# Expert weights of a mixture of experts fetched in rows of 8 KB instead of 2 KB

## The chip, the cores and the metric

The kernel runs on one core of one Trainium2 chip. The metric is the device time of one execution in microseconds, the median of several runs. The five engines are TensorE (PE; its weight loads are listed as PEld), VectorE (DVE), ScalarE (ACT), GpSimd (POOL) and SyncE (SP). SP issues nearly all transfers between the chip's memory and SBUF; they run on 16 DMA engines.

## What is computed

Two transformer blocks follow each other on 256 tokens of 1024 channels, in fp32. The first block ends in a mixture of 32 experts, two of them chosen for each token, and that is the part which matters here. Cut to it:

```python
h2 = modulate(rmsnorm(x, norm2_g), sh_m, sc_m)
# hier_moe: a group of 8 experts for each token, then the best 2 of its 8; gates of all others are 0
def body(acc, inp):
    wi, wo, ge = inp                       # (1024, 512), (256, 1024), (256,)
    a, u = jnp.split(t @ wi, 2, axis=-1)
    return acc + ((jax.nn.silu(a) * u) @ wo) * ge[:, None], None
y, _ = lax.scan(body, zeros, (w_expert_in, w_expert_out, gates))
x = x + gt_m * y
```

`w_expert_in` is (32, 1024, 512) and `w_expert_out` (32, 256, 1024) in fp32: 67 MB and 34 MB, all of which are read. Before this stands a token mixer (gated linear attention and pooling); behind it a second block with two FFNs, sparse attention, retention and a gate.

## The kernel before

**Stages.** The trace has them in this order: the modulation rows from `w_ada` and the projections of the first block (to about 140 us), its output projection `down(w_out)` and the routing (to about 197), the experts (to about 441), then the second block. In nearly all stages weights are read once, in tiles of 1 MB named `raw`, split into a rounded part `hi` (ACT, L197) and a rest `lo` (DVE, L198), and multiplied in two or three passes (L293 to L335).

**Memory.** SBUF is shared out by hand. `gp4` is a pool of eleven buffers of 4 KB a partition for temporaries (`t4`). Weight buffers lie in two regions, left and right, that `weight_pools` (L101) lays out anew between stages; a buffer of a new layout waits for the buffers of the old one on whose bytes it lies. `g4` in it are side buffers of the size of `gp4`'s, reached by `t4x`. `turn_of` takes the buffers of a kind in rotation.

**Experts.** Experts go in 11 units of three (the last has two). For each unit SP fetches twelve tiles `mw` of three experts by 128 rows by 512 columns, 6 KB a partition: eight tiles of `w_expert_in`, one for each block k of 128 channels, and four of `w_expert_out`, by column half n and block k (`unit_loads`, L704). Each row that is fetched is 2 KB. There are sixteen such buffers, 96 KB a partition. Five tiles of unit 0 are asked for early, from `ahead` (L775) in the middle of `down(w_out)`; the other eleven buffers lie over the left `raw`, `hi`, `lo` and `g4` of the stage before, `gta` in `g4` among them, which `x1_tile` reads. SP issues in order, so a load whose buffer isn't free holds all that stand behind it.

**Routing.** `x1_tile` and `logits` make the routing logits, DVE turns them into slots, and `gather_parts` (L825) writes the normed rows as a rounded part and a rest. Each expert takes up to 32 tokens. `gather` (L1027) multiplies the rows by a one-hot matrix `p4`, so that `xg` has the channels on partitions and the slots of a unit's four places side by side.

**One unit.** `in_proj` (L1065) multiplies, for each of eight k, four column groups of 32 (three experts and one place for an expert that overflows, chosen by a register). 32 of the trace's L1073 instructions are one half, kh. `act` is silu and product, `turn` transposes, `out_proj` (L1089) multiplies by the four `w_expert_out` tiles, `scatter` (L1098) spreads the result back over the tokens and adds it in PSUM. The gather of later units runs between. `scatter` of unit q stands behind `in_proj` of unit q+1. At q == 5 stands `beyond` (L973): a branch on whether an expert overflowed twice, passed by every engine.

**Behind the experts.** The left region gets `raw`, `hi`, `lo` and `g4` again, over the expert tiles' bytes, for the FFN (L1259), whose `hh` uses three side buffers.

Of the kernel before, what the change touches and what calls it, by code (L numbers as in the profile page):

```python
# [81 lines left out]
def body(ctx: ExitStack, tc: tile.TileContext, I, out, dbg=None):  # L82
# [6 lines left out]
    gp4 = ctx.enter_context(tc.tile_pool(name="gp4", bufs=11))  # L89
# [9 lines left out]
    SHAPES = {"g4": ([P, 1024], F32), "raw": ([P, 2048], F32), "hi": ([P, 1024], F32R), "lo": ([P, 1024], F32R), "mw": ([P, 3, 512], F32)}  # L99
# [24 lines left out]
    weight_pools("left", ("raw", 3), ("hi", 4), ("lo", 4), ("g4", 3))  # L124
# [127 lines left out]
    vrow = t1("vrow")[:44, :P]  # L252
# [6 lines left out]
    nc.scalar.dma_start(vrow[36:44, :], I["norm2_g"][0].rearrange("(k p) -> k p", p=P))  # L259
# [8 lines left out]
    vT = cp.tile([P, 44], F32, name="vT")  # L268
    sT = cp.tile([P, KD, 32], F32, name="sT")
    ps = bank()  # L270
    nc.tensor.transpose(ps[:, :44], vrow, ident[:44, :44])
    V.tensor_copy(vT, ps[:, :44])
# [7 lines left out]
    g2T = vT[:, 36:44]  # L280
# [418 lines left out]
    def unit_load(src, e):  # L699
        t = weight("mw")  # L700
        nc.sync.dma_start(t[:, :len(e)], src.rearrange("e p f -> p e f"))
        return t

    def unit_loads(u, some=12):  # L704
        e = experts[u]
        a, b = e[0], e[-1] + 1
        for k in range(KD):
            if k < some and (u, k) not in wi:
                wi[u, k] = unit_load(I["w_expert_in"][0, a:b, k * P:(k + 1) * P, :], e)
        for n in range(2):  # L710
            for k in range(2):
                if 8 + 2 * n + k < some and (u, k, n) not in wo:
                    wo[u, k, n] = unit_load(I["w_expert_out"][0, a:b, k * P:(k + 1) * P, n * 512:(n + 1) * 512], e)
# [3 lines left out]
    nc.sync.dma_start(wr[:, :, 0:4], I["w_router_group"][0].rearrange("(k p) f -> p k f", p=P))  # L717
    nc.sync.dma_start(wr[:, :, 8:40], I["w_router_expert"][0].rearrange("(k p) f -> p k f", p=P))
# [3 lines left out]
    def columns():  # L722
# [10 lines left out]
        for k in range(4):  # L733
            nc.tensor.transpose(pb[:, k * P:(k + 1) * P], row[:, k * P:(k + 1) * P], ident)
# [37 lines left out]
    weight_pools("right", ("mw", 5))  # L772
    pg = tok_panel((xL,), w_in, 1024, 512, (0, 0), ada_some)

    def ahead():  # L775
        columns()
        with after(asked):
            unit_loads(0, 5)
# [25 lines left out]
    def x1_tile(t):  # L804
# [3 lines left out]
        for n in range(2):  # L808
# [38 lines left out]
    weight_pools("left", ("mw", 4), ("mw", 5), ("mw", 2))  # L847
# [125 lines left out]
    def beyond():  # L973

        over = nc.values_load(mosti[0:1, 0:1], min_val=0, max_val=256)
        with tc.If(over > 0):  # L976
# [10 lines left out]
            with tc.For_i(0, NE, 1) as e:  # L987
                excess = nc.values_load(loads[0:1, bass.ds(e, 1)], min_val=0, max_val=256)
                with tc.If(excess > 0):
                    e_in, e_out = I["w_expert_in"][0, bass.ds(e, 1)][0], I["w_expert_out"][0, bass.ds(e, 1)][0]  # L990
                    pair_ = [bank(), bank()]
                    for c in range(2):
                        for m in range(2):
                            part = t4("part").rearrange("p (k f) -> p k f", k=KD)
                            c0 = 256 * c + P * m
                            nc.sync.dma_start(part, e_in[:, c0:c0 + P].rearrange("(k p) f -> p k f", p=P))
# [60 lines left out]
    def tiles_of(q, w):  # L1057

        if q == NU - 1:
# [5 lines left out]
    def in_proj(st_, q, kh):  # L1065
# [104 lines left out]
    weight_pools("left", ("raw", 5), ("hi", 6), ("lo", 6), ("g4", 3))  # L1170
# [88 lines left out]
    def ffn(norm, wg, wu, wdn):  # L1259

        hh, _ = blocks("hh", 22, F32R, 3)
# [196 lines left out]
    pT = [(t4x if i < 3 else t4)("pT").rearrange("p (h k q) -> p h k q", h=2, k=2) for i in range(4)]  # L1458
# [87 lines left out]
    yr = blocks2("yr", KD, 3)  # L1546
# [142 lines left out]
```

## Time and profile before

| | us |
|---|---|
| median of 3 runs (1098.5 to 1102.08) | 1098.74 |
| the profiled execution | 1098.91 |
| its span, first to last instruction | 1096.8 |

| engine | busy us | share |
|---|---|---|
| PE | 999.6 | 91% |
| PEld | 734.8 | 67% |
| DVE | 646.7 | 59% |
| ACT | 491.2 | 45% |

The profile page cuts the span into 40 slices of 27.4 us and gives for each the busy share of every engine, the clock that TensorE was granted, and what the DMA engines moved. A share for the whole span is an average over stages with different limits, so the stages have to be looked at one by one. Matmul instructions overlap in PE's pipeline; an instruction's duration is longer than the distance to the next one.

### The profile page before, as it was taken

The numbers are of one execution on the slowest core, as the hardware profiler recorded it, in microseconds if no ns is written. First come the engines' busy times: TensorE is split into PE (matmuls) and PEld (weight loads), VectorE is DVE, ScalarE is ACT, GpSimd is POOL, SyncE is SP. The second block draws the span as 40 slices with busy tenths as digits, with TensorE's granted clock in tenths as the row PEclk, the third lists the DMA queues.
The fourth block names the chain that finished last, engine by engine and source line by source line (L and its number), as shares of the span: only waits on it lengthen the run. The fifth ranks groups of instructions, "written<-read, shape, count | busy, mean of one in ns | idle before, by whom it ended". The sixth has DMA issues, their size and how long they took to land.

```text
span 1096.8 us, 15386 instructions
## 1 busy us (share of the span) xinstructions
PE 999.6 (91%) x5785; PEld 734.8 (67%) x5786; DVE 646.7 (59%) x1258; ACT 491.2 (45%) x873; POOL 5.7 (1%) x14
## 2 busy tenths in 40 slices
PE   4799997997778688799999999999999999999997
PEld 1586776442233132788888877787888788888886
DVE  3893865232112122976775499868659676775466
ACT  3544354321112011755554355675556455554353
POOL 1000000000000000000000000000000000000000
PEclk8899999999999989899999999999999999999999
DMA  9785886899999999776555633365367466565521
GB/s 374 270 298 182 304 289 220 307 385 386 387 383 386 386 387 381 239 238 193 184 219 192 192 117 114 118 209 167 102 206 253 128 196 223 159 222 197 190 81 39
DMA packets 152002, 260.60 MB, mean 238 GB/s; under 512 B 8444, under 2 KB 75240, under 8 KB 150648
## 3 DMA queue, kind: packets, MB, share of 16 engines
q1 hardware_dynamic: 151696, 259.32, 68.1%
q8 instruction: 48, 0.79, 0.3%
q10 hardware_dynamic: 232, 0.28, 0.1%
q14 instruction: 26, 0.21, 0.1%
HBM read 258.54 MB, written 1.05 MB: 237 GB/s over the span
## 4 chain that ended last, share of the span: by engine, by line
PE 59%; DMA 5%; DVE 4%; ACT 2%; issue 1%; DVEq 0%; ACTq 0%
PE mm L311 19%; PE mm L313 9%; PE acc L333 4%; PE acc L335 4%; PE acc L331 4%; DMA mw<-in_w_expert_in_dram 3%; PE acc L1237 2%; PE acc L1236 2%; PE acc L1244 2%; PE mm L1073 2%; PE mm L1095 2%; PE acc L294 1%; PE acc L295 1%; PE acc L293 1%; DMA mw<-in_w_expert_out_dram 1%; PE mm L1024 1%
## 5 line engine op out<-in xcount | busy, mean ns | idle before, releaser
L198 DVE TENSOR_TENSOR lo<-raw,hi 128x1024 fp32r<-128x1024 f32 (+1 forms) x240 | 287.2, 1204 | 159.6 <-ACT hi L197 157.0
L197 ACT CAST hi<-raw 128x1024 fp32r<-128x1024 f32 (+1 forms) x240 | 246.9, 1036 | 219.4 <-PE mm L311 93.6
L311 PE MATMUL mm<-xT,hi 128*128 128x512 f32 x832 | 211.9, 396 | 0.6 <-DVE rs L1516 0.6
L311 PEld LDWEIGHTS mm<-xT,hi 128*128 128x128 f32 x832 | 148.7, 188 | 28.5 <-DVE rs L1516 1.0
L313 PEld LDWEIGHTS mm<-xT,lo 128*128 128x128 f32 x832 | 110.6, 188 | 9.4
L313 PE MATMUL mm<-xT,lo 128*128 128x256 f32 x832 | 112.2, 277 | 0.0
L1073 PE MATMUL mm<-mw,xg 128*32 (+1 forms) x704 | 88.9, 600 | 21.6 <-DMA mw<-in_w_expert_in_dram 20.6
L1073 PEld LDWEIGHTS mm<-mw,xg 128*32 128x32 f32 x704 | 17.3, 109 | 71.9 <-DMA mw<-in_w_expert_in_dram 40.2
L295 PE MATMUL acc<-lo,xT 128*128 128x512 f32 x144 | 57.2, 402 | 1.9 <-DVE lo L198 1.9
L293 PE MATMUL acc<-hi,xT 128*128 128x512 f32 x144 | 58.3, 406 | 0.0
L294 PE MATMUL acc<-hi,xT 128*128 128x512 f32 x144 | 57.8, 401 | 0.0
L335 PE MATMUL acc<-lo,hh 128*128 128x512 f32 x176 | 56.3, 393 | 0.0
L333 PE MATMUL acc<-hi,hl 128*128 128x512 f32 x176 | 56.0, 392 | 0.0
L331 PE MATMUL acc<-hi,hh 128*128 128x512 f32 x176 | 55.9, 391 | 0.0
L1038 ACT ACTIVATE xg<-mm,shT,gmT 128x256 f32<-128x256 f32 (+1 forms) x48 | 23.4, 545 | 70.4 <-PE mm L1024 70.3
L1095 PE MATMUL mm<-mw,z 128*32 128x512 f32 (+1 forms) x352 | 46.5, 635 | 4.9 <-DMA mw<-in_w_expert_out_dram 4.4
L1103 DVE TENSOR_TENSOR og<-mm,gtm 128x512 f32<-128x512 f32 x22 | 15.2, 690 | 47.2 <-PE mm L1095 47.2
L1078 ACT ACTIVATE esg<-mm 128x256 f32<-128x256 f32 x11 | 4.2, 383 | 83.0 <-PE mm L1073 83.0
L1024 PE MATMUL mm<-p,xT 128*128 128x256 f32 (+1 forms) x192 | 34.7, 323 | 6.2 <-PEq L976 3.7
L1236 PE MATMUL acc<-hi,xT 128*128 128x256 f32 (+1 forms) x120 | 36.5, 330 | 2.3 <-ACT xT L197 2.3
L333 PEld LDWEIGHTS acc<-hi,hl 128*128 128x128 f32 x176 | 33.1, 188 | 7.3
L335 PEld LDWEIGHTS acc<-lo,hh 128*128 128x128 f32 x176 | 33.1, 188 | 7.2
(484 smaller groups left out, 1497.4 us busy)
## 6 DMA issues: line engine op xcount, KB each, us to landing
mw<-in_w_expert_in_dram SPq DMA_DIRECT2D x80, 768.0 KB, 13.0
raw<-in_w_in_dram SPq DMA_DIRECT2D x32, 1024.0 KB, 5.3
mw<-in_w_expert_out_dram SPq DMA_DIRECT2D x40, 768.0 KB, 13.1
raw<-in_w_ada_dram SPq DMA_DIRECT2D x24, 1024.0 KB, 8.4
raw<-in_ffn_w_gate_dram SPq DMA_DIRECT2D x22, 1024.0 KB, 5.5
raw<-in_ffn_w_up_dram SPq DMA_DIRECT2D x22, 1024.0 KB, 5.3
raw<-in_ffn_w_down_dram SPq DMA_DIRECT2D x22, 1024.0 KB, 4.9
raw<-in_w_out_dram SPq DMA_DIRECT2D x8, 1024.0 KB, 4.8
```

The source lines that it names most:

```text
L197: S.copy(hi, src)
L198: return V.tensor_tensor(lo, src, hi.bitcast(F32), op=ALU.subtract)
L293: mm(o, h_[k][:, c], hi[:, kk, z], start=k == starts, stop=False)
L294: mm(o, l_[k][:, c], hi[:, kk, z], start=False, stop=False)
L295: mm(o, h_[k][:, c], lo[:, kk, z], start=False, stop=k == stops)
L311: mm(pb, hi[:, k, :], x2[k], start=k == 0, stop=False, skip_group_check=True)
L313: mm(pb[:, 0:256], lo[:, k, :], x2[k][:, 0:256], start=False, stop=k == nk - 1, skip_group_check=True)
L331: mm(pa[t][n], hh[k][:, c], hi[:, 0, n * 512:(n + 1) * 512], start=k == seq[0], stop=False)
L333: mm(pa[t][n], hl[k][:, c], hi[:, 0, n * 512:(n + 1) * 512], start=False, stop=False)
L335: mm(pa[t][n], hh[k][:, c], lo[:, 0, n * 512:(n + 1) * 512], start=False, stop=k == seq[-1])
L1073: mm(st_["hp"][32 * i:32 * i + 32, :], xgs[q // 2][k // 4][:, k % 4, c:c + 32], w, start=k == 0, stop=k == KD - 1, skip_group_check=True)
L1095: mm(oo[n][r, :], st_["z"][:, k, r], w, start=k == 0, stop=k == 1, skip_group_check=True)
```

## The change

The tiles of expert weights become four times as large, 24 KB a partition, and there are four of them. Channels are renumbered inside each half of 512, so that partition p holds channels 4p to 4p+3: these are four neighbouring rows of `w_expert_in`, 8 KB in one piece. Inner units are renumbered alike, 2p and 2p+1, for `w_expert_out` (two rows of 4 KB in one piece). A unit has three tiles: two halves of `w_expert_in` and one of `w_expert_out`; only the second half of the last unit comes in four pieces of 512 columns. One tile instead of five small ones is asked for early.

All that meets the renumbered channels follows: the transposes of `xres` and of the modulation row take every fourth column, that of the hidden units every second, `gather_parts` writes its rows permuted in halves, the router weights come in two loads each, and `norm2_g` is fetched by its own transfer in place of eight rows of a transpose. `gp4` has one buffer less, the left region one side buffer more, and four lists of temporaries take one more tile from there.

```diff
-    gp4 = ctx.enter_context(tc.tile_pool(name="gp4", bufs=11))
+    gp4 = ctx.enter_context(tc.tile_pool(name="gp4", bufs=10))
...
-    SHAPES = {"g4": ([P, 1024], F32), "raw": ([P, 2048], F32), "hi": ([P, 1024], F32R), "lo": ([P, 1024], F32R), "mw": ([P, 3, 512], F32)}
+    SHAPES = {"g4": ([P, 1024], F32), "raw": ([P, 2048], F32), "hi": ([P, 1024], F32R), "lo": ([P, 1024], F32R), "mw": ([P, 3, 2 * D], F32)}
...
-    weight_pools("left", ("raw", 3), ("hi", 4), ("lo", 4), ("g4", 3))
+    weight_pools("left", ("raw", 3), ("hi", 4), ("lo", 4), ("g4", 4))
...
-    nc.scalar.dma_start(vrow[36:44, :], I["norm2_g"][0].rearrange("(k p) -> k p", p=P))
+    g2T = cp.tile([P, KD], F32, name="g2T")
+    nc.scalar.dma_start(g2T.rearrange("p (b k) -> p b k", k=4), I["norm2_g"][0].rearrange("(b p k) -> p b k", p=P, k=4))
...
-    def unit_load(src, e):
+    def unit_load(src, e, pieces=1):
         t = weight("mw")
-        nc.sync.dma_start(t[:, :len(e)], src.rearrange("e p f -> p e f"))
+        n = 2 * D // pieces
+        for c in range(0, 2 * D, n):
+            nc.sync.dma_start(t[:, :len(e), c:c + n], src[:, :, c:c + n])
         return t
...
-    def unit_loads(u, some=12):
+    def unit_loads(u, some=3):
+
         e = experts[u]
         a, b = e[0], e[-1] + 1
...
+        for h in range(2):
+            if h < some and (u, h) not in wi:
+                wi[u, h] = unit_load(I["w_expert_in"][0, a:b, 512 * h:512 * h + 512, :].rearrange(
+                    "e (p k) f -> p e (k f)", k=4), e, 4 if u == NU - 1 and h == 1 else 1)
+        if some > 2 and u not in wo:
+            wo[u] = unit_load(I["w_expert_out"][0, a:b].rearrange("e (p k) f -> p e (k f)", k=2), e)
+
+    def channels(k):
+
+        return slice(512 * (k // 4) + k % 4, 512 * (k // 4) + 512, 4)
...
+    for h in range(2):
+        for c, w in ((0, "w_router_group"), (8, "w_router_expert")):
+            n = I[w].shape[2]
+            nc.sync.dma_start(wr[:, 4 * h:4 * h + 4, c:c + n],
+                              I[w][0, 512 * h:512 * h + 512].rearrange("(p k) f -> p k f", k=4))
...
-    weight_pools("right", ("mw", 5))
+    weight_pools("right", ("mw", 1))
...
-            unit_loads(0, 5)
+            unit_loads(0, 1)
...
-                nc.tensor.transpose(pbs[n][:, kk * P:(kk + 1) * P], xres[:, t, k * P:(k + 1) * P], ident)
+                nc.tensor.transpose(pbs[n][:, kk * P:(kk + 1) * P], xres[:, t, channels(k)], ident)
...
-        S.activation(xrh[:, t, :], xres[:, t, :], AF.Copy, scale=rr[t])
-        V.scalar_tensor_tensor(xrl[:, t, :], xres[:, t, :], rr[t], xrh[:, t, :].bitcast(F32), op0=ALU.mult,
-                               op1=ALU.subtract)
+
+        for h in range(2):
+            c = slice(512 * h, 512 * h + 512)
+            src = xres[:, t, c].rearrange("p (c k) -> p k c", k=4)
+            S.activation(v4(xrh[:, t, c]), src, AF.Copy, scale=rr[t])
+            V.scalar_tensor_tensor(v4(xrl[:, t, c]), src, rr[t], v4(xrh[:, t, c]).bitcast(F32), op0=ALU.mult,
+                                   op1=ALU.subtract)
...
-    weight_pools("left", ("mw", 4), ("mw", 5), ("mw", 2))
+    weight_pools("left", ("mw", 1), ("mw", 2))
...
-            for i, w in enumerate(tiles_of(q, wi[q, k])):
+            for i, w in enumerate(tiles_of(q, wi[q, k // 4], (k % 4) * 512)):
...
-            nc.tensor.transpose(tp[:, k * P:(k + 1) * P], st_["sg"][:, k * P:(k + 1) * P], ident)
+            nc.tensor.transpose(tp[:, k * P:(k + 1) * P], st_["sg"][:, k:256:2], ident)
...
-                for i, w in enumerate(tiles_of(q, wo[q, k, n])):
+                for i, w in enumerate(tiles_of(q, wo[q], k * D + n * 512)):
...
-    weight_pools("left", ("raw", 5), ("hi", 6), ("lo", 6), ("g4", 3))
+    weight_pools("left", ("raw", 5), ("hi", 6), ("lo", 6), ("g4", 4))
...
-        hh, _ = blocks("hh", 22, F32R, 3)
+        hh, _ = blocks("hh", 22, F32R, 4)
```

## Rows read from the trace of the kernel before

**Rows 1.** The page's 40 slices of the span: PE busy tenths, DMA, GB/s.

```profile
PE   4799997997778688799999999999999999999997
...
DMA  9785886899999999776555633365367466565521
GB/s 374 270 298 182 304 289 220 307 385 386 387 383 386 386 387 381 239 238 193 184 219 192 192 117 114 118 209 167 102 206 253 128 196 223 159 222 197 190 81 39
```

**Rows 2.** Waits in 215:440: who waited for whom, us in total, times, longest.

```profile
PE mm L1073 <- DMA mw<-in_w_expert_in_dram: 20.6, 27, 1.2
```

**Rows 3.** Stretches: length, busy us (x instructions) by engine, PEclk, DMA share, GB/s.

```profile
16.00:24.00 8.00, 4.67 (x14) 2.54 (x15) 4.42 (x23) 6.90 (x15) 2.59 (x4) 0.62 1.02 430
16.00:28.00 12.00, 8.30 (x36) 4.04 (x36) 7.13 (x30) 8.05 (x16) 2.83 (x4) 0.72 1.02 427
114.00:120.00 6.00, 5.36 (x35) 4.03 (x34) 5.45 (x10) 2.00 (x2) 0.00 (x0) 1.00 1.03 412
230.00:300.00 70.00, 55.65 (x382) 20.96 (x378) 13.86 (x28) 10.97 (x21) 0.00 (x0) 0.98 1.05 387
320.00:420.00 100.00, 79.39 (x542) 28.80 (x538) 21.78 (x42) 15.96 (x31) 0.00 (x0) 0.97 1.05 387
440.00:446.00 6.00, 1.46 (x6) 0.88 (x6) 5.21 (x16) 5.19 (x17) 0.00 (x0) 0.89 1.10 348
...
380.00:400.00 20.00, 15.74 (x79) 5.70 (x80) 4.55 (x8) 4.16 (x9) 0.00 (x0) 0.83 1.05 388
```

**Rows 4.** Transfers: packets by size; an issue's start and us; KB and us to landing.

```profile
DMA packets 152002, 260.60 MB, mean 238 GB/s; under 512 B 8444, under 2 KB 75240, under 8 KB 150648
...
10.80 5.53 SPq L169 DMA_DIRECT2D raw<-in_w_ada_dram  x5
...
raw<-in_retmat_dram SPq DMA_DIRECT2D x1, 1024.0 KB, 4.8
...
DMA to landing us min/median/max: 5.4/12.9/14.7
```

**Rows 5.** PE in order of time, units 0 to 3: start us, us, instructions, count.

```profile
197.54 7.07 PE L1073 MATMUL mm<-mw,xg 128*32 x64
...
215.98 3.64 PE L1095 MATMUL mm<-mw,z 128*32 x32
...
227.38 2.76 PE L1073 MATMUL mm<-mw,xg 128*32 x24
...
247.30 1.07 PE L1073 MATMUL mm<-mw,xg 128*32 x8 [0.62 <-DMA mw<-in_w_expert_in_dram]
```

**Rows 6.** SP's queue in order of time, before and in the first units.

```profile
166.88 0.90 SPq L701 DMA_DIRECT2D mw<-in_w_expert_in_dram  x2
...
181.58 0.49 SPq L701 DMA_DIRECT2D mw<-in_w_expert_out_dram  x1
...
217.10 8.34 SPq L701 DMA_DIRECT2D mw<-in_w_expert_in_dram  x8
```

**Rows 7.** PE and SP around the branch at L976, in order of time.

```profile
310.32 1.06 PE L1073 MATMUL mm<-mw,xg 128*32 x8 [0.98 <-SPq L976]
...
314.83 8.88 SPq L701 DMA_DIRECT2D mw<-in_w_expert_in_dram  x8
...
315.06 2.05 PE L1024 MATMUL mm<-p,xT 128*128 128x256 f32 x8 [3.68 <-PEq L976]
```

**Rows 8.** PE in order of time: unit 8, then the last unit's end.

```profile
388.89 5.02 PE L1095 MATMUL mm<-mw,z 128*32 x24
...
433.10 2.78 PE L1095 MATMUL mm<-mw,z 128*32 128x512 f32 x24 [0.52 <-DVE z L1087]
...
440.17 0.73 PE L1110 MATMUL acc<-ol,back 128*128 128x512 f32 x2
```

**Rows 9.** DVE in order of time at the routing, token tile 0, then 1.

```profile
179.58 1.28 DVE L827 SCALAR_TENSOR_TENSOR xT<-xres,rmsz,xT 128x1024 fp32r<-128x1024 f32 x1 [0.69 <-ACT xT L826]
180.88 0.69 DVE L810 TENSOR_TENSOR om<-acc,ada 128x512 f32<-128x512 f32 x1
```

More of the change, by code (lines that the diff above doesn't have):

```diff
@@ L251, in body @@
     LF, LB, SF, SB, AFW = (tri[:, i * P:(i + 1) * P] for i in range(5))
-    vrow = t1("vrow")[:44, :P]
+    vrow = t1("vrow")[:36, :P]
     nc.scalar.dma_start(vrow[0:8, :], I["c"][0].rearrange("(k p) -> k p", p=P))
@@ L267, in body @@
     CI = cp.tile([P, 2, 32], F32R, name="CI")
-    vT = cp.tile([P, 44], F32, name="vT")
+    vT = cp.tile([P, 36], F32, name="vT")
     sT = cp.tile([P, KD, 32], F32, name="sT")
     ps = bank()
-    nc.tensor.transpose(ps[:, :44], vrow, ident[:44, :44])
-    V.tensor_copy(vT, ps[:, :44])
+    nc.tensor.transpose(ps[:, :36], vrow, ident[:36, :36])
+    V.tensor_copy(vT, ps[:, :36])
     V.tensor_copy(cstr, cst[:, 0:3, :])
@@ L279, in body @@
     rgnT = vT[:, 28:36]
-    g2T = vT[:, 36:44]
     def tok_mm(pa, lhs, w, c0, n, starts, stops, kh, skip=(0, 0)):
@@ L697, in body @@
     wi, wo = {}, {}
-    def unit_load(src, e):
+    def unit_load(src, e, pieces=1):
         t = weight("mw")
-        nc.sync.dma_start(t[:, :len(e)], src.rearrange("e p f -> p e f"))
+        n = 2 * D // pieces
+        for c in range(0, 2 * D, n):
+            nc.sync.dma_start(t[:, :len(e), c:c + n], src[:, :, c:c + n])
         return t
-    def unit_loads(u, some=12):
+    def unit_loads(u, some=3):
         e = experts[u]
         a, b = e[0], e[-1] + 1
[L707 to L713, printed above, removed]
+        for h in range(2):
[6 more added lines that the diff above has]
+        return slice(512 * (k // 4) + k % 4, 512 * (k // 4) + 512, 4)
     wr = t2("wr")[:, :KD * 40].rearrange("p (k f) -> p k f", k=KD)
     G.memset(wr, 0.0)
-    nc.sync.dma_start(wr[:, :, 0:4], I["w_router_group"][0].rearrange("(k p) f -> p k f", p=P))
-    nc.sync.dma_start(wr[:, :, 8:40], I["w_router_expert"][0].rearrange("(k p) f -> p k f", p=P))
+    for h in range(2):
[3 more added lines that the diff above has]
+                              I[w][0, 512 * h:512 * h + 512].rearrange("(p k) f -> p k f", k=4))
     shT, gmT, base = small(8, "shT", 1), small(8, "gmT", 1), small(40, "base", 1)
@@ L733, in columns @@
         for k in range(4):
-            nc.tensor.transpose(pb[:, k * P:(k + 1) * P], row[:, k * P:(k + 1) * P], ident)
+            nc.tensor.transpose(pb[:, k * P:(k + 1) * P], row[:, channels(k)], ident)
         cols = pb.rearrange("p (k j c) -> p c j k", j=4, c=32)
@@ L994, in beyond @@
                             part = t4("part").rearrange("p (k f) -> p k f", k=KD)
-                            c0 = 256 * c + P * m
-                            nc.sync.dma_start(part, e_in[:, c0:c0 + P].rearrange("(k p) f -> p k f", p=P))
+                            c0 = slice(256 * c + P * m, 256 * c + P * m + P)
+                            for h in range(2):
+                                nc.sync.dma_start(part[:, 4 * h:4 * h + 4, :], e_in[512 * h:512 * h + 512, c0]
+                                                  .rearrange("(p k) f -> p k f", k=4))
                             for k in range(KD):
@@ L1055, in way_back, with tiles_of @@
         return gs, back
-    def tiles_of(q, w):
+    def tiles_of(q, w, c0):
+        w = w[:, :, c0:c0 + 512]
         if q == NU - 1:
@@ L1455, in body @@
     rope_T(aqT, tok_panel((xL,), w2i, 0, 512)[0], 8, 32)
-    pT = [(t4x if i < 3 else t4)("pT").rearrange("p (h k q) -> p h k q", h=2, k=2) for i in range(4)]
+    pT = [(t4x if i < 4 else t4)("pT").rearrange("p (h k q) -> p h k q", h=2, k=2) for i in range(4)]
     for t in range(2):
@@ L1544, in pair @@
         return tiles[k2 // 2][:, 2 * (k2 % 2):2 * (k2 % 2) + 2, :]
-    yr = blocks2("yr", KD, 3)
+    yr = blocks2("yr", KD, 4)
     yr_ = [x.rearrange("p i c -> p (i c)") for x in yr]
@@ L1613, in body @@
     fg = row_bcast(t4x("fg"), I["final_norm_2"], D)
-    gt = [t4("gt"), t4("gt")]
+    gt = [t4x("gt"), t4("gt")]
     fss = small(6, "fss", 1).rearrange("p (t n) -> p t n", t=2)
```

## The prediction

> **What bounds the kernel now.** I read the 40 slices of the span first [rows 1]: two limits take turns. Through most of the span PE is at 9 tenths, but from about 220 to 440 us, the expert stage, the DMA line stands at 9 and 381 to 387 GB/s while PE falls to 6 to 8. So this stage, and this one alone, goes at the pace of the weight transfers. The table of waits says the same from PE's side: in 215:440 the expert matmuls of L1073 waited 27 times for `mw<-in_w_expert_in`, 20.6 us in all and none longer than 1.2 [rows 2]: each k tile comes just too late. Two long stretches show 387 GB/s at a DMA share of 1.05, PE busy 0.8 of the time [rows 3]. A change is worth something here if it moves the bytes faster or if it opens or closes gaps in that stream.
>
> **The rate by row length.** Other saturated stretches of this trace have other row lengths [rows 3]: 440:446, FFN panels of 256 columns (1 KB rows), 348 GB/s; 114:120, mostly 4 KB rows, 412; 16:28, 427. The last one is the five 1 MB loads of `w_ada` issued from 10.80 us on [rows 4], 2048 columns to a row, so 8 KB. The page counts 152002 packets, 150648 of them under 8 KB [rows 4], so 1354 of 8 KB or more: the eight `w_ada` loads alone have 1024 such rows, so a row of 8 KB does travel as one packet. In one order, 348, 387, 412, 427: longer rows are faster although all four stretches have the engines busy throughout.
>
> [...]
>
> **Removed and added: the stream.** A full tile becomes 3 x 128 rows x 8 KB = 3.146 MB, a unit three tiles, 9.437 MB as before. At 387 GB/s a tile takes 8.13 us and a unit 24.4; at 427, 7.37 and 22.1. I take 427, since it is measured on rows of the very length; the bounds are 387 (no gain) and 430, the first 8 us of the same loads (16:24) [rows 3].
>
> **Where the stream starts.** The same 96 KB of buffers hold four tiles instead of sixteen, and each is free only when its last reader is done. The early part, step by step: the first tile is asked for beside `w_out`, as five small ones are now. The second needs all three left `raw` buffers, free by about 168 us as now (SP issued small tiles there at 166.88) [rows 6]. The third and fourth lie over `hi`, `lo` and `gta`, which the last matmuls of L335 and x1_tile(1) hold: now SP gets through at 181.58 [rows 6], then too. They land before 198.5, and the fifth, h1 of unit 1, waits for the first half of in_proj(0): from 197.54 half of 7.07 us [rows 5], 201.1; with 2.3 us of latency (the 1 MB `retmat` load, 8 KB rows, landed in 4.8 us [rows 4]; 1.049 MB at 427 is 2.46) and 7.4 of transfer it lands at 210.8. in_proj(1) wants it near 209.8: 1 us of PE lost, out_proj(0) from 216.0 to 217 and its end from 219.6 to 220.4 [rows 5]. There the seventh tile (h0 of unit 2) is let in, behind which SP holds the rest; now SP goes on at 217.10 [rows 6]. So the gapless stream begins at 220.4 + 2.3 = 222.7, some 3 us later than now (217.10 + 2.3), with about as many bytes already in (six tiles, 18.9 MB). h0 of unit 2 lands at 230.1, where in_proj(2) now starts at 227.38 [rows 5]: PE idles there.
>
> **Where the stream ends.** From 222.7 on: 24 full tiles, 24 x 7.37 = 176.9; `fng`, 0.52 MB, 1.2; unit 10, two experts, two tiles of 2.10 MB at 4.91 and the four pieces of h1 that keep 2 KB rows, 5.42, together 15.2. That is 193.3 us, 416.0. One gap is added: at q == 5 every engine passes the branch of L976. Now PE ends in_proj(5) at 311.38 and goes on at 315.06, SP at 314.83, 3.45 us after PE's end [rows 7], and some 13 us of transfers asked for before (the median from issue to landing [rows 4]) cover it. After, only wo of unit 5 is asked for while SP stands there: h1 lands, PE needs 3.6 for its half, 3.45 for the branch, 2.3 until new bytes flow, 9.4 against the 7.4 of wo: 2.0 lost. So wo of unit 10 is in at 418.0.
>
> **The end of the stage.** Now out_proj(10) starts at 433.10 and the last scatter ends at 440.90: 7.8 us [rows 8], paced by PE with nothing waiting for weights. After, wo comes as one tile, so all of out_proj stands behind it, and PE may be 0.9 late from out_proj(9), scatter(9) and both halves of in_proj(10), which follow within 15 us: 418.0 + 0.9 + 7.8 = 426.7. The FFN panels follow the last weights in the queue as now and are wanted only after the norm behind the scatter, so their cover moves along. Gain: 440.9 - 426.7 = 14.2 us.
>
> **Can PE keep up?** From in_proj(2) to in_proj(3) is 227.38 to 247.30, 19.9 us [rows 5], with 2.3 us of idling in it: 17.6 us of work, 18.6 with the wait for esg that stays. That is under 22.1 and 16% spare. A tile let go late does not stop the stream soon: h0 is wanted again only 22 us after it landed, and PE needs 4 to 6. What is queued behind a late tile is all of SP; who waits is PE a unit later.
>
> **The small parts.** gather_parts becomes two DVE steps of 512 for one of 1024, 2 x 0.69 for 1.28 [rows 9], reading with a stride of 16 B; for token tile 0 L810 of x1_tile(1) is right behind it, so 0.1 us if the stride is free, 1.4 if it halves the rate; I take 0.2, since 512 and 1024 elements stand at 0.69 and 1.28 us, a time that goes by the elements. The strided transposes (two a unit, sixteen before the stage) change no count; zero to 0.5, in a stage with 3.5 us spare per unit. `g2T` adds 256 packets of 16 B to a start that is DMA bound: 0.2. The two more `wr` loads go out in the fourth slice, 82 to 110 us, at 182 GB/s with PE at 9 [rows 1], long before they are read: nothing. gp4 has one buffer less, and the tiles that are moved to the side pool (hh, pT, yr, gt) make up for it in the later stages; before 190 us and in the expert stage it is one less outright: 0 to 3, 0.5 taken, as I see no step there that needs the eleventh for long. Together 0.9.
>
> **Sum.** 14.2 - 0.9 = 13.3. The profiled execution took 1098.91 (span 1096.8 and 2.1 around it), 0.17 above the median of 1098.74, so nothing to correct: 1085.6.
>
> **Rivals.** 1. **The stream stays at 387 GB/s**, because memory or the cores' ports and not the packets set it; the coarse tiles then only cost. 82.3 MB at 387 is 212.7 us, from 222.7 to 435.4, with a smaller gap at the branch (1.3), 8.7 of tail and the small parts: 446.3, 5.4 late, 1104.3. It decides below 398 GB/s, where 82.3 MB fill just the time there is (440.9 less 222.7, 8.7, 2.0 and 0.9). Against it: 412 and 427 on the same engines; for it: all those stretches are short, and none reads three experts in turn. 0.10. 2. **PE becomes the bound**: waiting for whole tiles lets its clock fall. The granted clock was 0.83 in 380:400 [rows 3], after idling between tiles, and there 24 matmuls of L1095 took 5.02 us from 388.89 against 2.78 from 433.10 [rows 8]. One such group of 32 a unit adds 3.0 us, 21.6, still under 22.1; at two groups the unit is about 24.4 and the gain is gone. Halfway, 23.5 for eight units, costs 11: 1096. 0.10. 3. **Part of the rate only**, rows cut to 4 KB or the mix giving 412: 82.3 MB in 199.8 instead of 192.7, 1092.7; or the small parts at their upper bounds (4 more), 1090. 0.13. 4. Better: 430 GB/s (1.3 us), no gap at the branch (2.0), PE not late at the end (0.9), the small parts at nothing (0.9): 1080.5. 0.05.
>
> **How the numbers follow.** My forecast, 1082 to 1089, has 0.62. A measurement of this kernel tells 0.3%, 3.3 us, from no change. Faster: 0.62 + 0.13 + 0.05 and half of rival 2, 0.85. Slower: most of rival 1 and a little of 2, 0.09; the rest, 0.06, is the same. For 8 in 10 the range reaches from rival 4 to rival 2, 1080 to 1097, and leaves out rival 1.
>
> **What would show it.** DMA at 420 to 430 GB/s in the saturated stretch, packets of 8 KB or more up from 1354 by some 12000 (unit 10's pieces aside), units about 22 us apart at in_proj's starts, the last scatter near 427. A gap of 2 us in the DMA line behind L976, a PE wait before in_proj(2) of 2 to 3 us. Wrong would be: 387 GB/s with long packets (rival 1), DMA gaps in every unit with SP waiting for L1073 or L1095 (buffers too coarse), or PE without idling and a granted clock well under 0.9 there (rival 2).

## The result, and the profile after

| us | before | after |
|---|---|---|
| median of 9 runs each, taken together | 1099.3 (1096.54 to 1102.08) | 1091.38 (1089.36 to 1093.82) |
| profiled execution | 1098.91 | 1089.5 |
| its span | 1096.8 | 1087.2 |

The ratio is 0.993, 95% interval 0.9919 to 0.9941: 7.9 us faster. The forecast was 1085.6, with a range of 1080 to 1097; the time lies in it, but 2.4 us above the narrower 1082 to 1089. The direction and the main mechanism (longer rows, a faster stream) hold, and some 40% of the expected gain of 13.3 us is missing. The two profiled executions are 9.4 us apart; what follows is read from them.

The page's slices and packets of after:

```profile
PE   4799999898878787999999999999999999999996
...
DMA  9786866799989999665555542354367366555511
GB/s 377 275 293 190 305 235 251 293 422 419 422 361 420 422 420 370 211 207 183 205 213 192 157 165 97 130 189 155 117 205 260 120 213 200 173 215 210 187 68 39
DMA packets 114658, 260.59 MB, mean 240 GB/s; under 512 B 7205, under 2 KB 73993, under 8 KB 101273
```

Beside [rows 1] the expert stage is now at 419 to 422 GB/s where it stood at 381 to 387, but one slice of the stream stands out: 361 in the twelfth (299 to 326), where before had 383. The eighth (190 to 217), where the stream begins, has 293 for 307. Packets of 8 KB or more are 114658 - 101273 = 13385, against 1354 [rows 4], 12031 more, as forecast.

Stretches of after: length, busy us (x instructions) of PE, PEld, DVE, ACT and POOL, granted clock, DMA share, GB/s. Then who waited for weights in 215:435 (total us, times, longest).

```profile
184.00:192.00 8.00, 6.63 (x18) 3.94 (x17) 3.31 (x23) 4.64 (x5) 0.00 (x0) 0.50 1.01 428
196.00:204.00 8.00, 8.00 (x70) 4.85 (x72) 3.89 (x20) 5.20 (x10) 0.00 (x0) 0.93 0.07 26
206.00:210.00 4.00, 3.74 (x36) 1.31 (x32) 1.14 (x4) 0.38 (x1) 0.00 (x0) 1.00 0.99 420
240.00:300.00 60.00, 49.41 (x350) 19.93 (x346) 12.85 (x25) 10.74 (x21) 0.00 (x0) 0.94 1.01 420
306.00:314.00 8.00, 4.21 (x28) 2.79 (x21) 1.17 (x2) 0.80 (x2) 0.00 (x0) 0.74 0.60 219
308.00:310.00 2.00, 0.00 (x0) 0.00 (x0) 1.17 (x2) 0.16 (x1) 0.00 (x0) 0.95 0.75 299
310.00:312.00 2.00, 0.50 (x2) 0.53 (x3) 0.00 (x0) 0.00 (x0) 0.00 (x0) 0.50 0.17 66
340.00:380.00 40.00, 30.65 (x234) 11.61 (x226) 7.21 (x16) 5.39 (x12) 0.00 (x0) 0.96 1.01 421
...
PE mm L1089 <- DMA mw<-in_w_expert_in_dram: 9.0, 6, 3.8
PE mm L1111 <- DMA mw<-in_w_expert_out_dram: 4.9, 4, 1.5
```

The stream stands still until 204, runs at 420 from 206 on, loses 8 x (1 - 219/421) = 3.8 us in 306:314 and then runs at 421 again. PE waits for `w_expert_in` six times and 9.0 us instead of 27 times and 20.6 [rows 2], so less often but longer each time.

PE in order of time (start, us, instructions), L1089 being in_proj and L1111 out_proj; the last row is the end of the last scatter. Behind it, the first matmuls of the FFN, of after and then of before.

```profile
199.53 4.93 PE L1089 MATMUL mm<-mw,xg 128*32 x44
...
406.69 3.64 PE L1111 MATMUL mm<-mw,z 128*32 x32 [1.54 <-DMA mw<-in_w_expert_out_dram]
...
423.85 3.64 PE L1111 MATMUL mm<-mw,z 128*32 128x512 f32 x32 [0.52 <-DVE z L1103]
...
430.00 0.73 PE L1126 MATMUL acc<-ol,back 128*128 128x512 f32 x2
...
452.70 2.12 PE L311 MATMUL mm<-xT,hi 128*128 128x512 f32 x8
```

```profile
462.13 2.12 PE L311 MATMUL mm<-xT,hi 128*128 128x512 f32 x8
```

in_proj(0) starts at 199.53 against 197.54 [rows 5]. The last scatter ends at 430.73 against 440.90 [rows 8], 10.2 us earlier. The first L311 matmul of the FFN stands at 452.70 instead of 462.13, 9.4 earlier, and from it to the end of the span the kernels take 634.5 and 634.7 us. So the whole gain is made before 431, and 0.7 of it is lost between the last scatter and the FFN; why is open.

### The profile page after: what moved, and what is told of

Read it like the earlier page. It is cut to its first block, busy times and chain, and to the rows that moved or that the text cites. A ratio compares the mean times of both kernels' runs of the same rounds, so it can differ in the third digit from the quotient of the medians.

```text
span 1087.2 us, 15196 instructions
## 1 busy us (share of the span) xinstructions
PE 997.5 (92%) x5785; PEld 741.5 (68%) x5786; DVE 648.6 (60%) x1260; ACT 493.5 (45%) x875; POOL 5.7 (1%) x14
## 2 busy tenths in 40 slices
DMA packets 114658, 260.59 MB, mean 240 GB/s; under 512 B 7205, under 2 KB 73993, under 8 KB 101273
## 3 DMA queue, kind: packets, MB, share of 16 engines
HBM read 258.54 MB, written 1.05 MB: 239 GB/s over the span
## 4 chain that ended last, share of the span: by engine, by line
PE 58%; DMA 6%; DVE 4%; ACT 2%; issue 1%; SPq 0%; DVEq 0%; ACTq 0%
PE mm L311 20%; PE mm L313 9%; PE acc L333 4%; PE acc L335 4%; PE acc L331 4%; DMA mw<-in_w_expert_out_dram 3%; DMA mw<-in_w_expert_in_dram 2%; PE mm L1089 2%; PE acc L1253 2%; PE acc L1252 2%; PE acc L1260 2%; PE acc L294 1%; PE acc L295 1%; PE acc L293 1%; DMA raw<-in_ffn_w_up_dram 1%
## 5 line engine op out<-in xcount | busy, mean ns | idle before, releaser
L311 PE MATMUL mm<-xT,hi 128*128 128x512 f32 x832 | 211.8, 396 | 0.6 <-DVE rs L1532 0.6
L311 PEld LDWEIGHTS mm<-xT,hi 128*128 128x128 f32 x832 | 148.5, 188 | 28.6 <-DVE rs L1532 1.0
L1089 PE MATMUL mm<-mw,xg 128*32 (+1 forms) x704 | 85.8, 632 | 11.9 <-DMA mw<-in_w_expert_in_dram 10.9
L1089 PEld LDWEIGHTS mm<-mw,xg 128*32 128x32 f32 x704 | 22.2, 115 | 63.7 <-issue 52.4
L1111 PE MATMUL mm<-mw,z 128*32 128x512 f32 (+1 forms) x352 | 41.5, 601 | 5.5 <-DMA mw<-in_w_expert_out_dram 4.9
L331 PEld LDWEIGHTS acc<-hi,hh 128*128 128x128 f32 x176 | 32.9, 188 | 7.5
```

The costliest lines, as they stand in the source:

```text
L311: mm(pb, hi[:, k, :], x2[k], start=k == 0, stop=False, skip_group_check=True)
L331: mm(pa[t][n], hh[k][:, c], hi[:, 0, n * 512:(n + 1) * 512], start=k == seq[0], stop=False)
L1089: mm(st_["hp"][32 * i:32 * i + 32, :], xgs[q // 2][k // 4][:, k % 4, c:c + 32], w, start=k == 0, stop=k == KD - 1, skip_group_check=True)
```

## The experiments

My theory was the prediction's, with what the trace of after had added: rows of 8 KB make the rate, the branch makes the hole, the strided steps make in_proj(0) late. The rivals: the gain comes from larger tiles and not from longer rows; the hole is PE's standstill and costs nothing; PE sets the pace, so that nothing done to the stream shows. A difference under about 2 us between kernels of this list isn't told apart by their times alone.

**The changed kernel again**, on the chip of rows_2kb, two_tiles_ahead and plain_gather, which were run beside it.

> The changed kernel as it is, beside which the next three are read on the same chip. 0.993 of the kernel before, as measured; last scatter near 431 us, 420 GB/s in the expert stage, a hole of some 5 us in the transfers behind the branch at q == 5, in_proj(0) near 199.5 us.

1090.3 us, ratio 0.9906 (0.9891 to 0.9921). Its profile repeats that of after: 421 GB/s in 240:300, 336 in 300:320, in_proj(0) at 200.11, the last scatter's end at 431.36.

**Rows of 2 KB in the same tiles.** Only the cut of each load changes.

```diff
-                    "e (p k) f -> p e (k f)", k=4), e, 4 if u == NU - 1 and h == 1 else 1)
+                    "e (p k) f -> p e (k f)", k=4), e, 4)
...
-            wo[u] = unit_load(I["w_expert_out"][0, a:b].rearrange("e (p k) f -> p e (k f)", k=2), e)
+            wo[u] = unit_load(I["w_expert_out"][0, a:b].rearrange("e (p k) f -> p e (k f)", k=2), e, 4)
```

> The changed kernel with every expert tile fetched in four pieces of 512 columns: rows of 2 KB again, everything else (four large tiles, permuted channels, pools) as changed. Theory 1, the row length sets the rate and the rate the stage: 387 GB/s, 8.13 us a tile for 7.48; 26 tiles from 205 us on make 17 us more, last scatter near 447, time near 1108, slower than the kernel before. Rival, the gain is from fewer and larger tiles and fewer waits: 420 GB/s in the four-piece form too or no loss from 387, time near 1091.

1113.17 us, ratio 1.0112 (1.0093 to 1.0131). **Rows of 4 KB**, the same with 2 in place of the 4 and the last unit's second half left in four pieces:

> The changed kernel with every full tile asked for in two pieces of 1024 columns, rows of 4 KB; tiles, buffers and waits as in the changed kernel. By the rows of 114:120 (412 GB/s, mostly 4 KB rows) between the 386 of 2 KB and the 420 of 8 KB: 405 to 412 in 240:300, 7.7 us a tile, 24 tiles 4 to 6 us more, the last scatter near 436 and 1095 to 1096. If the rate has its step between 2 and 4 KB and not more beyond: 419 or more and within 1.5 us of the changed kernel.

1097.87 us, ratio 0.9982 (0.9967 to 0.9996). The stretch 240:300 of the two, 2 KB first (columns as above):

```profile
240.00:300.00 60.00, 46.38 (x316) 20.60 (x318) 10.53 (x22) 9.59 (x19) 0.00 (x0) 0.91 1.05 386
```

```profile
240.00:300.00 60.00, 45.83 (x333) 19.14 (x332) 12.86 (x25) 10.98 (x21) 0.00 (x0) 0.97 1.03 409
```

With one tile, one buffer and one matmul order for all three, the rate goes 386, 409, 420 with the length of the row: the first rival falls. It also shows what the coarse tiles cost by themselves: with 2 KB rows the kernel is 12.5 us slower than the one before on that chip (1100.68), at the same 386 to 387 GB/s. Longer rows give 22.9 back (1113.2 to 1090.3), and the change's gain is the difference.

**One load for each expert.** Each tile is asked for by three loads of 1.05 MB.

```diff
-            nc.sync.dma_start(t[:, :len(e), c:c + n], src[:, :, c:c + n])
+            for i in range(len(e)):
+                nc.sync.dma_start(t[:, i, c:c + n], src[:, i, c:c + n])
```

> The changed kernel, with each tile asked for by three loads of 1.05 MB (one expert each, 128 rows of 8 KB) instead of one of 3.15 MB; rows and bytes are the same. If the 420 to 421 GB/s against the 427 of the w_ada loads come from the three experts in one load (three rows a partition in turn): 427 in 240:300 and 340:360, 7.37 us a tile, 26 tiles 2.9 us less, the last scatter near 428.5 and 1088. If it is the state of the chip in this stage (PE, DVE and ACT at work beside it): 420 again, within 1 us of the changed kernel, 1090 to 1091.

1090.17 us, ratio 0.9903 (0.9886 to 0.9919), 420 GB/s in 240:300. Three experts in one load are not why 427 wasn't reached. That the work of the other engines beside the stream is, as the expectation's second case has it, isn't shown by this.

**Without the branch.** The two lines `if q == 5: beyond()` are left out, of the changed kernel and of the one before.

> The changed kernel with the call of beyond() left out: the overflow path (L986 to L1029) and the branch ahead of it are not there, which for this data leaves out no work that is done. Theory (SP, once in the branch, passes its semaphores 7.5 us apart, at 289.1, 296.6, 304.0 and 311.5, so it stands there until all four tiles that it has asked for have landed, and the stream runs dry behind it): without the branch 300:320 goes at 420 GB/s instead of 336 to 338, all later tiles land 4 us earlier, the last scatter ends near 427 instead of 430.7 to 431.4, and the time is about 1086.5. Rival (from wo of unit 9 on PE sets the end, and the stage has so little room that the hole is made up for before): the last scatter within 1.5 us of 431, 1089.5 or more.

> The kernel before with the call of beyond() left out, likewise no work that is done for this data. Theory: with sixteen small tiles SP comes to the branch at 308 with the last transfers already asked for and the stream dips only to 308 GB/s in 316:318, 0.4 us of transfers; PE's 3.7 us at the branch lie beside the stream. So it gains 0.4 to 1 us: 1098.5 to 1099.5 where before stands near 1099.5, and the branch costs the changed kernel 4 us more than this one. Rival (the branch's price is PE's standstill, the same in both kernels): it gains 3.5 to 4 us, 1095.5 to 1096.

The changed kernel gains 4.3 us on its 1090.3: 1085.95, ratio to before 0.9864 (0.9847 to 0.9881). Before gains 1.3, by the interval 0.2 to 2.5: 1098.6, ratio 0.9988 (0.9977 to 0.9998). That rests on the medians alone: the profiled execution of before_no_branch took 1100.07, and its last scatter ends at 442.39, later than the 440.90 of before. The stretch 300:320 without the branch is whole:

```profile
300.00:320.00 20.00, 14.33 (x110) 6.51 (x106) 4.34 (x9) 3.66 (x7) 0.00 (x0) 1.00 1.01 419
```

The last scatter ends at 427.92, 2.8 us before that of after and 3.4 before that of the changed kernel again. The two kernels that ran beside it and keep the branch, one_load_per_expert and branch_loads_elsewhere, stand at 1090.2 and 1090.3. So the branch costs the changed kernel more than it cost before, 4.3 us for 1.3. It is the largest gap in the stream, though the forecast had 2.0 us for it. What SP does in it is told by its semaphore waits at the branch's line, each with its instant. Of after (SP reaches the branch at 288.0):

```profile
L989 SPq EVENT_SEMAPHORE  x1: 17/17/17, 289.1 to 289.1; - x1
L989 SPq EVENT_SEMAPHORE  x1: 17/17/17, 296.6 to 296.6; - x1
L989 SPq EVENT_SEMAPHORE  x1: 17/17/17, 304.0 to 304.0; - x1
L989 SPq EVENT_SEMAPHORE  x4: 17/17/17, 311.5 to 311.7; - x4
```

They stand 7.4 to 7.5 us apart, one tile at 420 GB/s. SP waits in the branch for the landing of the four tiles that it has asked for, the last being wo of unit 5, and asks for the next one at 312.14. 308:310 still moves 299 GB/s and 310:312 only 66: the stream runs dry, as if it had stopped at 309.4, wherever PE stands.

**Two tiles asked for ahead of the branch.** `unit_loads(6, 2)` stands before `beyond()`.

> The changed kernel with the two w_expert_in tiles of unit 6 asked for ahead of the branch at q == 5 instead of behind it. Theory: the transfers stand still from 309.4 to 314.2 only because SP waits at the branch, and as all later tiles follow without a hole this comes out at the end in full: no hole, last scatter 4 to 5 us earlier, 1087. Rival: PE sets the pace of units 5 to 7 (in_proj(6) found its tiles there without a wait), so the bytes come earlier and PE doesn't: 1 us or less, 1090.5 or more.

1090.55 us, ratio 0.9912 (0.9898 to 0.9927): no gain that can be told. The number is the rival's, but not for its reason, for the hole is still there. SP's waits in the branch, and the stretches of the old place and the new:

```profile
L989 SPq EVENT_SEMAPHORE  x5: 17/17/17, 301.5 to 301.8; - x5
L989 SPq EVENT_SEMAPHORE  x1: 17/17/17, 309.2 to 309.2; - x1
L989 SPq EVENT_SEMAPHORE  x1: 17/17/17, 316.7 to 316.7; - x1
L989 SPq EVENT_SEMAPHORE  x2: 17/17/17, 324.1 to 324.2; - x2
...
300.00:316.00 16.00, 10.35 (x70) 5.79 (x74) 2.35 (x6) 2.42 (x5) 0.00 (x0) 0.79 1.02 421
316.00:328.00 12.00, 10.32 (x82) 3.24 (x78) 3.43 (x7) 1.24 (x2) 0.00 (x0) 0.86 0.76 286
```

The hole has moved to the landing of the last tile asked for, 324, with its size kept: 12 x (1 - 286/421) = 3.8 us. PE left the branch at 309.98 in this run, 14 us before SP, so SP doesn't wait for PE here, nor PE for SP.

**The branch's own loads on another queue.** The loads inside `beyond` (which don't run for this data) are asked for by ACT.

> The changed kernel, with the two kinds of loads inside beyond() asked for by ACT's queue instead of SP's; the branch stays, and its loads do not run for this data. If SP waits in the branch for its transfers because that path asks for transfers of its own on the same queue: SP goes through with PE at about 309 to 311 without the four waits, asks for h0 of unit 6 at once when its slot is free, 300:320 is near 400 GB/s or more, the last scatter ends 1.5 to 3 us earlier and the time is 1087.5 to 1089. If any branch makes SP wait for what it has in flight: the four events 7.5 us apart stay, 336 GB/s in 300:320, 1090.5 as now.

1090.29 us, ratio 0.9911 (0.9896 to 0.9927), the four waits at 288.3, 295.8, 303.3 and 310.7, and 324 GB/s in 300:320. It is not the loads inside that make SP wait.

**One tile from POOL's queue.** POOL passes the branch at 198.6 in after and has no transfer of its own on the way.

```diff
+                    nc.gpsimd if (u, h) == (6, 0) else None)
```

> The changed kernel, with one of its 29 full tiles, the first of unit 6, asked for by POOL's queue instead of SP's. POOL has nothing to do in the stage and goes through the branch at 198; two_tiles_ahead showed the tile's buffer free at 291. Theory (each engine waits in the branch for the transfers that it has asked for itself): the tile is asked for near 291 to 293 and flows from 309 to 317, while SP still waits for wo of unit 5 until 311; no hole in 306:320, 415 GB/s or more, PE still stands 3 to 4 us at the branch beside the stream, the last scatter ends near 427 as without the branch, 1086 to 1087.5. Rival (the branch holds the end of all transfers together, or POOL's way to ask for a load is slow): a hole of 3 us or more in 304:330 and 1089 or more.

> pool_load and plain_gather in one: gather_parts writes in the order of the channels and the matmuls of L1039 read every fourth column. If the two gains are of different places (the start and the branch), this is the faster of all that keep the branch: in_proj(0) at 196.5, the last scatter near 426, 1085 to 1086.5. If the stream alone sets the pace behind unit 1, the start gives nothing: within 0.7 us of pool_load.

Both miss their theory: 1091.04, ratio 0.992 (0.9906 to 0.9934), and 1091.11, ratio 0.9927 (0.9914 to 0.9939); the second is within 0.1 us of the first, as if the earlier start gave nothing. Their profiles can't be set beside each other for that: in_proj(0) starts at 199.93 and 197.18, and the last scatter ends at 433.60 and 429.35, but in pool_load out_proj(9) took 6.40 us for the 3.64 of after, at a granted clock of 0.83 in 400:420 (1.00 in after). Of pool_load, SP's waits in the branch (one line further down in it), PE at the second half of in_proj(5), and two stretches:

```profile
L990 SPq EVENT_SEMAPHORE  x1: 17/17/17, 296.8 to 296.8; - x1
L990 SPq EVENT_SEMAPHORE  x1: 17/17/17, 310.1 to 310.1; - x1
L990 SPq EVENT_SEMAPHORE  x4: 17/17/17, 319.3 to 319.5; - x4
...
310.17 2.79 PE L1090 MATMUL mm<-mw,xg 128*32 x12 [8.35 <-SPq L990]
...
300.00:316.00 16.00, 6.94 (x44) 1.73 (x36) 0.75 (x3) 0.37 (x1) 0.00 (x0) 0.68 1.01 421
316.00:324.00 8.00, 5.20 (x46) 3.15 (x50) 2.29 (x4) 2.17 (x6) 0.00 (x0) 1.00 0.57 206
```

POOL asked at 293.96, and from then on h1 of unit 5 took 13.3 us to follow the tile before it instead of 7.5. With two queues at work the stream moved 421 GB/s in 300:316, no more than with one, so the early tile put back the one that PE needed next (8.35 us of waiting) and was done before SP's own last one, at 319.3. By the trace's record it landed at 313.5, and SP's waits have no step there: SP waited for its own transfers alone. The hole came behind 319.3. My theory of the wait stood; what fell was the tacit assumption that a tile asked for later also arrives later.

**POOL's tile late.** With plain_gather (below) as its base, unit 6 takes its buffers in the order h1, wo, h0, so that POOL's tile waits for the buffer of h1 of unit 5.

```diff
+        for h in (1, 2, 0) if u == 6 else range(3):
```

> plain_gather with the loads of unit 6 in the order of buffers h1, wo, h0, and h0 asked for by POOL: h0 then takes the buffer of h1 of unit 5, which is free when the second half of in_proj(5) is done, 306 to 308. What pool_load showed (two queues share the engines, so the early load of POOL put h1 of unit 5 back by 6 us and ended before SP's own) cannot happen: SP has 2 us or less to bring in at that time. Theory: POOL asks at 307 to 308, bytes from 310, h0 lands at 317 to 318, and SP, let go at about 311 to 313, has h1 and wo of unit 6 behind it: the hole shrinks from about 4 us to about 2, 300:320 at 375 to 390 GB/s instead of 337, and the time is 1087 to 1088 against plain_gather's 1089.5. Rival (the buffers are now in another order, so that a later tile waits for a later reader, or PE waits for h0 of unit 6 after all): a new hole behind 320 or PE waits of 3 us or more in 317:340, 1089 to 1091.

POOL asked at 308.83, and the stretch is:

```profile
300.00:320.00 20.00, 14.64 (x107) 7.14 (x99) 3.33 (x8) 3.04 (x6) 0.88 (x1) 0.91 0.94 379
```

The hole went from 4 to 2 us as expected, with no new one behind, and the last scatter ends at 428.40, 1.9 us before that of plain_gather. This 1.9 isn't the hole's: plain_gather lost 1.5 us at the end, where its out_proj(9) took 5.08 us for 3.64 (below), while here in_proj(0) started 1.7 us later (198.33 for 196.65) and out_proj(9) 0.5 us earlier (404.35 for 404.83), 2.2 us made up between them. The time was 1088.13, but the kernel before ran at 1097.62 on that chip, and the ratio, 0.9904 (0.9886 to 0.9923), is that of plain_gather. The profile shows the smaller hole; a gain in time over plain_gather isn't shown.

**gather_parts in the order of the channels.** The rows are written unpermuted, and the gather's matmuls read every fourth column of them as weights instead.

```diff
-                mm(pb[:, kk * 256:kk * 256 + w], (xrh, xrl)[i][:, t, k * P:(k + 1) * P], places[b][:, t, :],
+                mm(pb[:, kk * 256:kk * 256 + w], (xrh, xrl)[i][:, t, channels(k)], places[b][:, t, :],
```

> The changed kernel with gather_parts as before (one contiguous step of 1024 each on ACT and DVE); the stride of 4 is put on the stationary operand of the gather matmuls instead. Theory: the strided reads take 1.15 us for 512 elements where contiguous ones take 0.69, hold x1_tile(1) back on DVE so that PE idles 2.0 us, and its granted clock falls to 0.50 in 184:188; undone, clock 1.00 there, in_proj(0) at about 197.5 instead of 199.5, the stream and the stage's end 2 us earlier, 1089.4. Rival: the late start is covered, since the transfers bound the stage: in_proj(0) earlier, time the same within 0.5 us. If strided weight loads are slow, the 32 gather matmuls take over 5.4 us and eat the gain.

1089.49 us, ratio 0.9903 (0.9887 to 0.9918), no more than the changed kernel's in its interval, though in_proj(0) starts at 196.65. First of before, then of after and of this kernel, the rows of x1's second addition (DVE), of `gather_parts`, of L853 (after alone), of the gather's matmuls and of their weight loads (min/median/max ns); of this kernel also out_proj(9). Last, rows of two_tiles_ahead, whose routing is that of after:

```profile
173.54 1.28 DVE L811 TENSOR_TENSOR xres<-xres,om 128x512 f32<-128x512 f32 x2
192.04 5.57 PE L1024 MATMUL mm<-p,xT 128*128 128x256 f32 x32 [2.54 <-DVE p L863]
```

```profile
172.57 1.28 DVE L820 TENSOR_TENSOR xres<-xres,om 128x512 f32<-128x512 f32 x2
177.53 2.31 ACT L839 ACTIVATE xT<-xres,rmsz 128x512 fp32r<-128x512 f32 x2
178.78 1.15 DVE L840 SCALAR_TENSOR_TENSOR xT<-xres,rmsz,xT 128x512 fp32r<-128x512 f32 x1 [0.75 <-ACT xT L839]
184.16 2.06 PE L853 MATMUL mm<-grow,gsel 128*128 128x512 f32 x2
194.25 5.35 PE L1039 MATMUL mm<-p,xT 128*128 128x256 f32 x32 [2.54 <-DVE p L876]
...
L1039 PEld LDWEIGHTS mm<-p,xT x192: 187/192/338, 194.2 to 404.8; 128*128 128x128 f32 x192
```

```profile
170.43 1.28 DVE L820 TENSOR_TENSOR xres<-xres,om 128x512 f32<-128x512 f32 x2
175.40 1.14 ACT L835 ACTIVATE xT<-xres,rmsz 128x1024 fp32r<-128x1024 f32 x1
188.97 7.75 PE L1035 MATMUL mm<-p,xT 128*128 128x256 f32 x32 [2.54 <-DVE p L872]
...
L1035 PEld LDWEIGHTS mm<-p,xT x192: 307/329/339, 188.9 to 404.4; 128*128 128x128 f32 x192
...
404.83 5.08 PE L1107 MATMUL mm<-mw,z 128*32 x32
```

```profile
172.40 1.28 DVE L820 TENSOR_TENSOR xres<-xres,om 128x512 f32<-128x512 f32 x2
183.69 1.10 PE L853 MATMUL mm<-grow,gsel 128*128 128x512 f32 x2
192.08 5.36 PE L1039 MATMUL mm<-p,xT 128*128 128x256 f32 x32 [2.54 <-DVE p L876]
...
404.50 3.64 PE L1111 MATMUL mm<-mw,z 128*32 x32 [1.06 <-DMA mw<-in_w_expert_out_dram]
```

From that addition to the first gather matmul are 18.5 us before, 21.7 after and 18.5 here: with the 16 B stride on ACT and DVE the routing chain is 3.2 us longer in after. In two_tiles_ahead, with the same stride, it is 19.7: there PE's clock stayed up (a pair of L853 took 1.10 us for the 2.06 of after). So the stride takes 1.2 us of the 3.2 and the clock 2.0. But here the stride has only gone to PE, whose weight loads take 329 ns instead of 192, and its gather 7.75 us instead of 5.35. Net, in_proj(0) comes 26.2 us after the addition, against 27.0 after and 24.0 before. The other 2.1 us of its earlier start were there at the addition already. Nor is an early start covered by the stream: out_proj(9) starts at 404.83 against 406.69 in after, but takes 5.08 us for 3.64, and the last scatter ends at 430.32, only 0.4 us earlier. The profile of two_tiles_ahead, with a hole like that of after, shows it whole: in_proj(0), out_proj(9), the end of the last scatter (428.53) and the profiled execution (1087.33) are all 2.2 us earlier than in after. Its other three executions, 1090.48 to 1090.67, weren't profiled.

## Why the prediction was right, and where it was wrong

**The rate: right in kind, 1.5% too high.** The step that failed is the 427, taken from a 12 us stretch of `w_ada`; the long stretches of after, and the one with its loads cut by experts, give 420 to 421. On the way to wo of unit 9, some 76 MB, that is 2.8 us. The row length isn't at fault: expert tiles in the same rows ran at 428 GB/s in the 8 us of 184:192 of after. A short stretch gave the higher rate in both kernels; what the long stage lacks beside it is open. The trace of before allows another price: 348 GB/s at 1 KB and 387 at 2 KB [rows 3] are 47.1 and 84.7 ns for a packet on one of the 16 engines, so 9.5 ns and 37.6 ns for each KB, and a packet of 8 KB comes to 310 ns, 422 GB/s. That is nearer, in part by luck, since the 348 are from 6 us only.

**The stream's start: too late.** The prediction held SP at h0 of unit 2 until out_proj(0). That tile took the buffer of h0 of unit 1 instead, in the pool of two, which is free after half of in_proj(1), and SP asked for it at 211.25. From 204.9 the stream had no gap, and at 222.7 it was some 20.1 MB in (four tiles, and 17.8 us at 421 GB/s) instead of 18.9: 2.9 us better. The expected wait before in_proj(2) isn't there; the one at h1 of unit 1 is, 1.95 us for an expected 1.

**The branch: the wrong mechanism.** The prediction had SP held until PE comes through and bytes 2.3 us later, a hole of 2.0. In the changed kernel SP waits for its own transfers, whoever else has passed, and the hole is 3.8. In [rows 7] SP's 314.83 was read as following PE. It followed landings: before has four such waits, at 308.6, 310.3, 312.3 and 314.4, a small tile apart. By the trace's record two more small tiles landed behind the one waited for last, at 316.4 and 318.4, so the stream there fell only to 308 GB/s in 316:318, some 0.4 us; why SP didn't wait for these two is open. The coarse tiles made the hole, and the bound was put on the wrong cause.

**The landing of a tile: left out.** What waited for a tile in these traces was let go when the slowest of the 16 engines was done with it. For wo of unit 5 in after the trace records the engines' ends from 309.6 to 311.5, and SP is let go at 311.5; at full flow the bytes would have been in at 309.4. For wo of unit 9 the ends go from 404.9 to 406.6. These 2 us are in no term behind the stream's start: the prediction's 2.3 us of latency, from an issue to its landing, all stood ahead of the first byte, and the last byte counted as the landing. Small tiles have the same spread (308.4 to 310.3 for one of before), so it isn't the coarse tiles that made it.

**The sum.** With the prediction's steps wo of unit 9 would be in at 418.0 - 15.2 = 402.8; PE's wait for it ended at 406.6. The start gives -2.9, the rate +2.8, the hole +1.8 (3.8 for 2.0) and the landing +2.0, together 3.7. This sum is worked out from the trace; of its terms the runs showed the rate and the hole by themselves. It is the sum of the profiled execution, 1089.5 for the forecast 1085.6. The median, 1091.38, is another 1.9 us later, and no profile shows where these lie; that profiles of these kernels differ by some 2 us through PE's clock alone (next paragraphs) makes the clock likely, not shown. The median is close to rival 3's 1092.7, for rows that go at 412; with 420 to 421 measured, its condition didn't hold. The forecast's 1085.6 is 13.3 less than the profiled 1098.91; from the median of before it would be 1085.4.

**The end of the stage: right.** From the start of out_proj(9) to the end of the last scatter are 24.0 us in after, and 24.0 to 24.1 in the changed kernel again, in no_branch, pool_load_plain, two_tiles_ahead, branch_loads_elsewhere and late_pool_load: PE's own pace, in which wo of unit 10 is no longer awaited. From the prediction's 402.8 this ends at 426.8, where it had 426.7.

**Rival 2, a slower clock by waiting, has a part at the two ends.** Ahead of the stage the clock has the 2.0 us of the next paragraph, though not by waiting for tiles. At the end, where out_proj(9) ran slower after its wait (6.44 us in one_load_per_expert and 6.40 in pool_load, against 3.64; granted clock 0.83 in 400:420 of both, 1.00 in after), the stretch of 24.0 takes 26.5. In the middle it doesn't decide: 240:300 has PE 49.4 of 60 us busy at a granted 0.94 and the DMA share at 1.01.

**The small parts: gather_parts mis-sized.** 0.2 was taken, 0.1 to 1.4 were the bounds. The stride doubles ACT's time (two steps 2.31 for 1.14) and takes DVE 1.15 us for 0.69 in a step of 512 elements. By itself it lengthens the routing chain by 1.2 us, near the upper bound, as the one profile of two_tiles_ahead shows. The chain of after grew by 3.2. The other 2.0 are PE's clock, which has no term in the prediction: the granted clock was 1.00 in 184:188 of before and 0.50 in 184:192 of after, where PE had just idled 2.0 us for `xres` (1.2 before), and four matmuls of L853 took 4.1 us for 2.2. In two_tiles_ahead, with the same strided steps, it stayed at 1.00 until 188, and in_proj(0) began at 197.36. It fell in eight of the nine profiles with strided steps, where L853's four matmuls took 3.7 to 4.1 us, and in none of the five without, where PE idled 1.2 us or less at that place; what decided it in the ninth, with the same 2.0 us of idling, is open. Since the stream restarts only when in_proj(0) lets its first tile go, this delays the stream; it is inside the 204.9 above. The strided transposes are in plain_gather too, whose chain is as short as that of before (18.5 us): they cost nothing there. `gp4` and `hh` show nothing behind the FFN's first matmul, where both kernels take the same time; nor is a loss seen ahead of the routing, since the addition comes at 172.57 in after and 173.54 in before.

**Rival 1 was underpriced.** rows_2kb has that rival's rate, 386 GB/s, and its coarse tiles, and took 1113.2 for the 1104.3 given. Its hole behind the branch is 6.6 us (318:330 moves 175 GB/s) where 1.3 was taken, and the landing was missing there as well.

## What to carry to other kernels

Turn rates into time per packet (here 9.3 ns and 37.8 ns for each KB), and don't trust a short stretch to the last per cent, even one with rows of just the right length: expert tiles in rows of 8 KB ran at 428 GB/s for 8 us and at 420 to 421 for 40 to 60. When many small transfers become a few large ones, list the points where a queue has to run empty. Here one branch took 3.8 us of the stream from the large tiles and 0.4 from the small ones. Count a tile as there when its slowest engine is done, here 1.7 to 1.9 us after the first, not when its bytes are in on average. A stride that an edit moves from one engine to another is not gone: from ACT and DVE to PE it came back as 329 ns for 192 in a weight load. It can also cost beyond its own steps: here PE idled 0.8 us longer, and the fall of its clock that went with it in eight of nine profiles cost more than the stride itself (2.0 us for 1.2 in after).

## What the runs showed of the hardware that was not expected

**Time per packet.** 386, 409 and 420.5 GB/s at 2, 4 and 8 KB (240:300 of rows_2kb and rows_4kb, the long stretches of after) are 84.9, 160.2 and 311.7 ns a packet and engine. A line through the first and the last, 9.3 ns and 37.8 ns for each KB, gives 160.5 at 4 KB and 47.1 at 1 KB, where 348 GB/s [rows 3] are 47.1. Its limit for endless rows is 433 GB/s, an estimate from these rows. Against that limit the runs show 11% less with rows of 2 KB and 6% less with rows of 4 KB.

**The branch.** SP waited there for the transfers that it had asked for itself, in the changed kernel for all of them (four landings, 289.1 to 311.5), in the kernel before not for the last two. PE stood 3.8 us in it, as before (3.7), and left it 14 us ahead of SP in one run.

**The spread of the engines' ends.** In before and after the 16 engines ended one tile over 1.7 to 1.9 us, large or small, and who waited for it was let go with the last. In rows_2kb a load of the same stage had its ends over 3.9 us (315.5 to 319.4).

**Strided reads.** Reading every fourth fp32 element took ACT 2.31 us for 1.14 (1024 elements), DVE 1.15 us for 0.69 in a step of 512 elements, and PE 329 ns for 192 in a weight load.
